# Roots of the q/kv statistics on ScalarE, and a new order of the stage's last steps

## The chip, the cores and the metric

The kernel runs on one core of one Trainium2 chip. The metric is device time in microseconds (us) for one execution of the whole program. Five engines work from queues of their own, each in its order: TensorE (PE: matmuls and transposes), VectorE (DVE), ScalarE (ACT), GpSimd (POOL), and SyncE (SP), which issues DMAs. An instruction that needs the result of another engine waits at the head of its queue, and everything behind it on that engine waits with it.

## The reference

One layer with two parallel groups of heads that read the same normalised input. There are 1024 latent tokens and 128 context tokens, 9 tiles of 128 rows; the context is tile 8. The part that the change touches makes, for each tile, a low-rank query `c_q` (256 wide), a key/value latent `c_kv` (128) and a rotary key (64):

```python
def _rmsnorm(x, g):
    xf = x.astype(jnp.float32)
    y = xf * lax.rsqrt(jnp.mean(xf * xf, axis=-1, keepdims=True) + EPS)
    return (y * g.astype(jnp.float32)).astype(x.dtype)
...
    u, v, g_a, c_q, c_kv, k_rope, g_b = _split_in(h @ w_in)
    a_out = _chunk_mlp(u, v, w_s, b_s, g_v) * jax.nn.silu(g_a)
    q = (_rmsnorm(c_q, q_norm_g) @ w_uq).reshape(B, L, MLA_HEADS, QK_NOPE + QK_ROPE)
    ckv = _rmsnorm(c_kv, kv_norm_g)
```

Keys and values come from `ckv`; attention is a softmax over latent keys and 256 cached context keys for latent tokens, and over the context's own 128 keys for tile 8. The kernel folds the key expansion into the query, so that the normalised latent itself serves as key, and it applies the root of `c_q` later, as the scale of the softmax (`scl`, `nscl`).

## The kernel before

Matmuls are made in three passes on operands that are split into a high part and the low rest. So nearly every result in PSUM is evicted twice: ACT copies the high part, then DVE subtracts it from the PSUM value to give the low part (`lo_of`, line 104). Here such a pair is called an eviction; `kch`/`kcl`, `krh`/`krl`, `cqh`/`cql` are such pairs.

The q/kv stage (lines 986 to 1040) stands between the channel matmuls and attention. Its engines run in the order in which the code issues instructions, and that order is written out by hand: `run((cost, fn))` calls a step's function and moves a planned clock on by its cost; `later(dt, fn)` puts a function on a list with a due time, and `catch_up` issues what is due, in order of due times, before the next step. An eviction that is due earlier on this planned clock thus stands earlier in its engine's queue, whenever its input really comes. `need(...)` issues what is on the list until the named thing has been made.

For each tile t, eight `z_chunk` steps (24 matmuls) accumulate `c_q`, `c_kv` and the rotary key in one PSUM bank. The last one calls `z_stats` (line 824). There ACT copies the bank to SBUF (`z`, line 869), two ACT activations square and sum it (lines 832 and 833), `scales` (line 835) computes 1/sqrt of both sums, and `apply` writes the normalised latent `kvn` and the scales. Before the change, 1/sqrt is an integer first guess and three Newton steps, twelve small DVE operations one after another (`rsqrt_ops`, line 109). For the last tile (`last`, t = 8) squares and scales have later due times (2.6 and 4.2 instead of 0.35 and 1.6), and the operations a wider gap.

Beside the chunks of tile t run steps of earlier tiles: `cq_transpose(t-1)`, `q_rope(t-2)` with its rotation, `q_rope_T(t-3)`, `fold`, and `q_nope(g, h)`, the queries of three tiles and one head. After tile 8's last chunk comes the list of lines 1022 to 1038: transposes of the keys of tiles 0 to 7 (`keys(0, 4, kind)`, `keys(4, 4, kind)`; kind 0 is the latent, 1 the rotary key), `cq_transpose(8)`, `q_rope_T(6)` and `(7)`, `q_rope(8)`, the last query group `q_nope(2, 0..3)`, and tile 8's own `q_rope_T(8)` and `keys(8, 1, kind)`.

PSUM has eight banks. In this stage two belong to a pool `pst` (tag `t`: key transposes of tiles 0 to 3 and of tile 8, `q_rope_T(8)`), six to a pool `psa` (tag `acc`: nearly all else). Within a pool the next tile takes the bank that was given back first, and its first matmul waits for the last reader of the tile before. In attention the six banks go to `o` and the context's own score (one bank), to `s2` (one), and to two score tiles of two banks each. The first score (line 1087, head 0 of tile 0) thus takes over two banks of the stage's last `acc` tiles. The scores of tile 0 need the keys of tiles 0 to 7 and the cached context, not those of tile 8; these are read by the context's own score, which is the fifth step of attention.

The activation tables: ACT works with one set of functions at a time, and the program has a table load (`ACT_TABLE_LOAD`) ahead of each activation whose function is not in the set in force. `warm_e` (line 989) is an activation whose result nobody reads; it is the first ACT instruction of the stage's code and has no input but a constant.

Of the kernel before, what the change touches and what calls it, by code (L numbers as in the profile page):

```python
# [9 lines left out]
F32 = mybir.dt.float32  # L10
# [3 lines left out]
AF = mybir.ActivationFunctionType  # L14
# [4 lines left out]
P = 128  # L19
NT = 9  # L20
# [66 lines left out]
def tile_hymba_step(ctx: ExitStack, tc: tile.TileContext, I, O):  # L87
# [21 lines left out]
    def rsqrt_ops(pool, v, n, tag):  # L109
        r = pool.tile([P, n], F32, tag=f"{tag}r", name=f"{tag}r")  # L110
        t = pool.tile([P, n], F32, tag=f"{tag}t", name=f"{tag}t")
        w = pool.tile([P, n], F32, tag=f"{tag}w", name=f"{tag}w")
        ops = [
            lambda: V.tensor_scalar(t.bitcast(I32), v.bitcast(I32), 1, None, op0=ALU.logical_shift_right),
            lambda: V.tensor_scalar(r.bitcast(I32), t.bitcast(I32), -1, 0x5F3759DF, op0=ALU.mult, op1=ALU.add),
            lambda: V.tensor_scalar(w, v, -0.5, None, op0=ALU.mult),
        ]
        for _ in range(3):
            if n == 1:
                ops.append(lambda: V.scalar_tensor_tensor(t, r, r, w, op0=ALU.mult, op1=ALU.mult))  # L120
            else:
                ops.append(lambda: V.tensor_tensor(t, r, r, op=ALU.mult))
                ops.append(lambda: V.tensor_tensor(t, t, w, op=ALU.mult))
            ops.append(lambda: V.scalar_tensor_tensor(r, t, 1.5, r, op0=ALU.add, op1=ALU.mult))
        return r, ops
# [33 lines left out]
    def later(dt, fn):  # L159
        waiting.append((now[0] + dt, fn))  # L160
        waiting.sort(key=lambda w: w[0])

    def catch_up(until):
        at_ = now[0]
        while waiting and waiting[0][0] <= until:
            due, fn = waiting.pop(0)
            now[0] = due
            fn()
        now[0] = at_
# [29 lines left out]
    def run(step):  # L199
        catch_up(now[0])  # L200
        step[1]()
        now[0] += step[0]
# [621 lines left out]
    def z_stats(t, ps):  # L824
        zt[t] = zp.tile([P, 448], F32, tag="z", name=f"z{t}", bufs=2)
        zs = zt[t]
        ssz = sm.tile([P, 2], F32, tag="ssz", name=f"ssz{t}")
        kr = zs[:, 384:448]

        def squares():  # L830
            j1 = sm.tile([P, 256], BF16, tag="j1", name=f"j1{t}", bufs=1)
            S.activation(j1, ps[:, 0:256], AF.Square, accum_out=ssz[:, 0:1])
            S.activation(j1[:, :128], ps[:, 256:384], AF.Square, accum_out=ssz[:, 1:2])

        def scales():
            v = sm.tile([P, 2], F32, tag="zv", name=f"zv{t}")
            r, ops = rsqrt_ops(sm, v, 2, "z")
            V.tensor_scalar(v[:, 0:1], ssz[:, 0:1], 1.0 / 256.0, EPS, op0=ALU.mult, op1=ALU.add)
            V.tensor_scalar(v[:, 1:2], ssz[:, 1:2], 1.0 / 128.0, EPS, op0=ALU.mult, op1=ALU.add)
            gap = 0.28 if t == NT - 1 else 0.2  # L840
            for i, op in enumerate(ops):
                later(gap * i, op)
            later(gap * len(ops), lambda: apply(r))

        def apply(r):
            V.scalar_tensor_tensor(kvn[:, t, :], zs[:, 256:384], r[:, 1:2], kvg, op0=ALU.mult, op1=ALU.mult)
            V.tensor_scalar(scl[:, t : t + 1], r[:, 0:1], ATTN_SCALE, None, op0=ALU.mult)
            V.tensor_scalar(nscl[:, t : t + 1], r[:, 0:1], -ATTN_SCALE, None, op0=ALU.mult)
            made.add(("k", t))
            if t == NS:  # L850
                nc.sync.dma_start(O["new_ckv"], kvn[:, t, :])
                nc.sync.dma_start(O["new_krope"], kr)

        def rope_key():
            if t < NS:
                t1 = sm.tile([P, 64], F32, tag="kr1", name=f"kr1{t}")
                t2 = sm.tile([P, 64], F32, tag="kr2", name=f"kr2{t}")
                G.tensor_tensor(t1, kr, rope[:, 0, t, :], op=ALU.mult)
                G.tensor_tensor(t2[:, 0:32], kr[:, 32:64], rope[:, 1, t, 0:32], op=ALU.mult)
                G.tensor_tensor(t2[:, 32:64], kr[:, 0:32], rope[:, 1, t, 32:64], op=ALU.mult)  # L860
                G.tensor_tensor(krd[:, t, 0, :], t1, t2, op=ALU.add)
                G.tensor_tensor(krd[:, t, 1, :], t1, t2, op=ALU.add)
            else:
                G.tensor_copy(krd[:, t, 0, :], kr)
                G.tensor_copy(krd[:, t, 1, :], kr)


        last = t == NT - 1
        later(0.3, lambda: S.copy(zs, ps[:, :448]))
        later(2.6 if last else 0.35, squares)  # L870
        later(0.9, rope_key)
        later(4.2 if last else 1.6, scales)

    def cq_transpose(t):
        last = t == NT - 1
# [18 lines left out]
    def q_nope(g, h):  # L894
        need(*[("cq", t) for t in range(3 * g, 3 * g + 3)])
        ps = psa.tile([P, 512], F32, tag="acc", name=f"qn{g}{h}")
        gc = slice(g * GW, (g + 1) * GW)
        passes3(ps[:, :GW], [(wfh[:, q, h, :], wfl[:, q, h, :], cqh[:, q, gc], cql[:, q, gc]) for q in range(2)])
        later(1.2, lambda: S.copy(qnh[g][:, h, :], ps[:, :GW]))
        later(1.75, lambda: lo_of(qnl[g][:, h, :], ps[:, :GW], qnh[g][:, h, :]))  # L900
# [85 lines left out]
    NOPES = {4: [(0, 0)], 5: [(0, 1), (0, 2)], 6: [(0, 3)], 7: [(1, 0), (1, 1)], 8: [(1, 2), (1, 3)]}  # L986
    with tc.manual_schedule(engines=engines):
        warm_e = sm.tile([P, 1], F32, tag="warm", name="warm_e", bufs=1)
        S.activation(warm_e, ones[:, 0:1], AF.Exp)
        rope_weights()  # L990
        for t in range(NT):
            beside = []
            if t >= 2:
                beside.append((0.75, lambda t=t: q_rope(t - 2)))
            beside += [(1.05, lambda n=n: q_nope(*n)) for n in NOPES.get(t, [])[:1]]
            if t >= 1:
                beside.append((0.25, lambda t=t: cq_transpose(t - 1)))
            if 1 <= t < 5:
                beside.append((0.45, lambda t=t: fold(t - 1)))
            if t >= 3:  # L1000
                beside.append((0.45, lambda t=t: q_rope_T(t - 3)))
            beside += [(1.05, lambda n=n: q_nope(*n)) for n in NOPES.get(t, [])[1:]]
            if t == NT - 1:
                beside.append((0.75, lambda: q_rope(t - 1)))
            merged([(0.62, lambda t=t, k=k: z_chunk(t, k)) for k in range(NK)], beside)
        closed(c_w1)
        c_kv, kv = opened("kv", side="left")
        kch = kv.tile([P, 11 * P], F32R, tag="kch", name="kch")
        kcl = kv.tile([P, 11 * P], F32R, tag="kcl", name="kcl")
        krh = kv.tile([P, 11 * P], F32R, tag="krh", name="krh")  # L1010
        krl = kv.tile([P, 11 * P], F32R, tag="krl", name="krl")
        vh = kv.tile([P, 11, P], F32R, tag="vh", name="vh")
        vl = kv.tile([P, 11, P], F32R, tag="vl", name="vl")
        for i, (dh, dl) in enumerate(((kch, kcl), (krh, krl))):
            later(0.3, lambda dh=dh, i=i: pool_copy(dh[:, CTX0:], ctxr[:, i, :]))
            later(0.3, lambda dh=dh, dl=dl, i=i: G.tensor_tensor(dl[:, CTX0:], ctxr[:, i, :], f32(dh[:, CTX0:]), op=ALU.subtract))
        cv = [v_[:, 9:, :].rearrange("p a r -> p (a r)") for v_ in (vh, vl)]
        later(11.0, lambda: pool_copy(cv[0], ctxr[:, 2, :]))
        later(11.0, lambda: G.tensor_tensor(cv[1], ctxr[:, 2, :], f32(cv[0]), op=ALU.subtract))
        for t0, c in ((8, 1), (0, 4), (4, 4)):  # L1020
            later(11.5, lambda t0=t0, c=c: values(t0, c))
        for cost, fn in (
            (0.45, lambda: keys(0, 4, 0)),
            (0.45, lambda: keys(0, 4, 1)),
            (0.25, lambda: cq_transpose(8)),
            (0.45, lambda: keys(4, 4, 0)),
            (0.45, lambda: keys(4, 4, 1)),
            (0.45, lambda: q_rope_T(6)),
            (0.45, lambda: q_rope_T(7)),
            (0.75, lambda: q_rope(8)),  # L1030
            (1.05, lambda: q_nope(2, 0)),
            (1.05, lambda: q_nope(2, 1)),
            (1.05, lambda: q_nope(2, 2)),
            (0.15, lambda: keys(8, 1, 1)),
            (1.05, lambda: q_nope(2, 3)),
            (0.25, lambda: q_rope_T(8)),
            (0.15, lambda: keys(8, 1, 0)),
        ):
            run((cost, fn))
        catch_up(1e9)  # L1040
    closed(c_zp)
    closed(c_pa)
# [565 lines left out]
```

## Time and profile before

| | us |
|---|---|
| median of three runs | 635.0 (634.12 to 635.34) |
| the profiled execution | 633.38 |
| its span, first to last instruction | 631.6 |
| q/kv stage on PE, first chunk to first score | 247.56 to 325.29 |

The mean granted clock of TensorE over the span is 0.995 of full speed. The profile is one execution; a row of a timeline has start, duration, engine, line of the kernel, operation, output<-inputs, shape and count, and in brackets the engine's idle time just before with what ended it. Durations of successive matmuls overlap, so the pace of PE is read from start to start. A low part has line 104 whatever it belongs to, so it is told by its tile names; `area` holds the finished queries. A row of `x2` or `x4` joins neighbours of one form.

### The profile page before, as it was taken

The page shows a single profiled execution, that of the slowest core. Times are in us where ns is not written, and L with a number is a line of the kernel's source. Part 1 is how long each engine was busy: PE and PEld are TensorE (multiplying, and loading weights), DVE is VectorE, ACT ScalarE, POOL GpSimd, SP SyncE. Part 2 cuts the span into 40 slices and gives each one's busy share as a digit, 9 for nine tenths or more (in the row PEclk, how much of TensorE's full clock was granted, in tenths as well). Part 3 has the DMA queues.
Part 4 walks back from the last instruction along what each step waited for, and adds up shares of the span by engine and source line. Part 5 has one row for each costly group of instructions (what it writes and reads, how often), then busy time and mean ns, then how long its engine had stood idle before and what let it go on. Part 6 is the DMA issues. An engine that isn't in the chain of part 4 may idle for free.

```text
span 631.6 us, 9907 instructions
## 1 busy us (share of the span) xinstructions
PE 614.2 (97%) x3733; PEld 557.1 (88%) x3733; DVE 366.5 (58%) x907; ACT 259.4 (41%) x615; POOL 181.8 (29%) x217
## 2 busy tenths in 40 slices
PE   7999999999999999999979999999999999999995
PEld 6677889999999999999967999999999988888884
DVE  3666447048556200667866665776766755487655
ACT  8456753112111111455646556555555543132212
POOL 2545123247532510433443221332222341000001
PEclk9999999999999999999989999999999999999999
DMA  8993100042322320000010000000101012524311
GB/s 324 353 356 107 34 0 2 1 141 109 113 92 72 110 88 13 25 2 1 2 39 1 2 2 0 1 1 35 34 1 34 33 68 87 181 100 134 104 64 66
DMA packets 17120, 46.32 MB, mean 73 GB/s; under 512 B 1953, under 2 KB 6449, under 8 KB 17073
## 3 DMA queue, kind: packets, MB, share of 16 engines
q1 hardware_dynamic: 16928, 45.51, 21.1%
q8 instruction: 29, 0.48, 0.3%
q10 hardware_dynamic: 144, 0.20, 0.1%
q14 instruction: 19, 0.15, 0.1%
HBM read 40.87 MB, written 4.83 MB: 72 GB/s over the span
## 4 chain that ended last, share of the span: by engine, by line
PE 91%; DVE 4%; ACT 2%; DMA 1%; issue 1%; SPq 0%; ACTq 0%
PE tp L670 6%; PE tp L150 6%; PE tp L152 6%; PE tp L151 6%; PE pT L1134 5%; PE w L1383 5%; PE w L1382 5%; PE w L1381 5%; PE s L1087 3%; PE o L1158 3%; PE o L1160 3%; PE s L1088 3%; PE s L1089 3%; PE s L1090 3%; PE o L1159 3%; PE s L1091 3%
## 5 line engine op out<-in xcount | busy, mean ns | idle before, releaser
L104 DVE TENSOR_TENSOR pl<-pT,ph 128x512 fp32r<-128x512 f32 x81 | 55.5, 687 | 48.0 <-ACT ph L1138 47.8
L1078 POOL TENSOR_SCALAR e<-e,rs 128x1280 f32<-128x1280 f32 x32 | 43.0, 1343 | 134.1 <-DVE rs L1077 116.3
L152 PE MATMUL tp<-area,w2l 128*128 128x384 f32 x216 | 72.5, 336 | 0.0
L150 PE MATMUL tp<-area,w2h 128*128 128x384 f32 x216 | 72.5, 336 | 0.0
L151 PE MATMUL tp<-area,w2h 128*128 128x384 f32 x216 | 72.5, 336 | 0.0
L1072 ACT ACTIVATE e<-s,nb,scl 128x256 f32<-128x256 f32 x64 | 56.1, 881 | 37.6 <-DVE nb L1066 37.6
L1138 ACT CAST ph<-pT 128x512 fp32r<-128x512 f32 x80 | 45.4, 589 | 43.5 <-PE pT L1134 40.6
L1134 PE MATMUL pT<-ident,e 128*128 128x128 f32 x320 | 47.8, 272 | 0.7 <-DVE pl L104 0.7
L1158 PE MATMUL o<-ph,vh 128*128 128x256 f32 x160 | 47.8, 299 | 0.0
L104 DVE TENSOR_TENSOR w2l<-w2r,w2h 128x1024 fp32r<-128x1024 f32 x12 | 20.2, 1685 | 46.1 <-POOL w2h L107 46.1
L1160 PE MATMUL o<-ph,vl 128*128 128x256 f32 x160 | 44.9, 281 | 0.0
L1159 PE MATMUL o<-pl,vh 128*128 128x256 f32 x160 | 44.7, 280 | 0.0
L1383 PE MATMUL w<-area,ml 128*128 128x512 f32 (+1 forms) x114 | 43.2, 379 | 0.0
L1134 PEld LDWEIGHTS pT<-ident,e 128*128 128x128 f32 x320 | 37.5, 140 | 4.4 <-DVE pl L104 1.5
L1062 DVE TENSOR_REDUCE m<-s 128x1 f32<-128x1024 f32 x32 | 38.9, 1216 | 4.0 <-PE s L1091 4.0
L150 PEld LDWEIGHTS tp<-area,w2h 128*128 128x128 f32 x216 | 40.5, 188 | 0.6 <-issue 0.5
L151 PEld LDWEIGHTS tp<-area,w2h 128*128 128x128 f32 x216 | 40.5, 188 | 0.2
L152 PEld LDWEIGHTS tp<-area,w2l 128*128 128x128 f32 x216 | 40.5, 188 | 0.0
L1087 PE MATMUL s<-kch,area 128*128 128x512 f32 (+2 forms) x100 | 39.5, 395 | 0.6 <-DVE area L104 0.6
L670 PE MATMUL tp<-area,w2h 128*128 128x384 f32 x144 | 37.4, 340 | 0.0
L1089 PE MATMUL s<-kch,area 128*128 128x512 f32 (+2 forms) x100 | 35.8, 358 | 0.0
L1088 PE MATMUL s<-kcl,area 128*128 128x512 f32 (+2 forms) x100 | 35.7, 357 | 0.0
(309 smaller groups left out, 1590.0 us busy)
## 6 DMA issues: line engine op xcount, KB each, us to landing
ada<-in_ada_ss SPq DMA_DIRECT2D x16, 512.0 KB, 10.9
w2r<-in_w_t SPq DMA_DIRECT2D x12, 512.0 KB, 4.3
xr<-in_x SPq DMA_DIRECT2D x9, 512.0 KB, 5.1
adag<-in_ada_g SPq DMA_DIRECT2D x8, 512.0 KB
wor<-in_w_o SPq DMA_DIRECT2D x8, 512.0 KB, 3.4
out_y<-y SPq DMA_DIRECT2D x8, 512.0 KB, 2.7
x<-in_x SPq DMA_DIRECT2D x6, 512.0 KB, 8.7
wvr<-in_w_v SPq DMA_DIRECT2D x8, 256.0 KB, 8.6
```

The source lines that it names most:

```text
L104: V.tensor_tensor(lo, src, f32(hi), op=ALU.subtract)
L150: T.matmul(ps, wh, xh, start=j == 0, stop=False)
L151: T.matmul(ps, wh, xl, start=False, stop=False)
L152: T.matmul(ps, wl, xh, start=False, stop=j == n - 1)
L670: T.matmul(tps[i, g][:, :GW], w_[i][:, k, :], x_[k, g], start=k == 0 and j == 0, stop=k == NK - 1 and j == 2)
L1072: S.activation(e[:, sl], src, AF.Exp, bias=nb, scale=scl[:, t : t + 1], accum_out=su[:, i : i + 1])
L1087: T.matmul(ps, qh_, kch[:, sl], start=True, stop=False)
L1134: T.transpose(ps[:, w : w + P], es[t, h][:, c * P : (c + 1) * P], ident)
L1158: T.matmul(o, vh[:, kt, :], ph[:, sl], start=c == 0, stop=False)
L1159: T.matmul(o, vh[:, kt, :], pl[:, sl], start=False, stop=False)
L1160: T.matmul(o, vl[:, kt, :], ph[:, sl], start=False, stop=c == n - 1)
L1383: T.matmul(ps, b, woh[k][:, c0:c1], start=False, stop=k == NK - 1)
```

## The change

In `scales`, ACT takes the square roots of both sums (one activation each, with the mean's factor as scale and EPS as bias), and DVE takes the reciprocal and makes one Newton step on it, four operations instead of twelve. The last tile's squares and scales lose their later due times; scales are due at 1.5 instead of 1.6 for all tiles. In the list after the last chunk, `keys(8, 1, 1)` and `keys(8, 1, 0)` go from behind `q_nope(2, 2)` and from the end to a place behind `q_nope(2, 0)`, and `q_rope_T(8)` goes ahead of `q_nope(2, 3)`. The unread activation at the stage's start asks for Sqrt instead of Exp, and a second one at its end asks for Exp.

```diff
@@ scales @@
             v = sm.tile([P, 2], F32, tag="zv", name=f"zv{t}")
-            r, ops = rsqrt_ops(sm, v, 2, "z")
-            V.tensor_scalar(v[:, 0:1], ssz[:, 0:1], 1.0 / 256.0, EPS, op0=ALU.mult, op1=ALU.add)
-            V.tensor_scalar(v[:, 1:2], ssz[:, 1:2], 1.0 / 128.0, EPS, op0=ALU.mult, op1=ALU.add)
-            gap = 0.28 if t == NT - 1 else 0.2
-            for i, op in enumerate(ops):
-                later(gap * i, op)
-            later(gap * len(ops), lambda: apply(r))
+            root = sm.tile([P, 2], F32, tag="zw", name=f"zw{t}")
+            r = sm.tile([P, 2], F32, tag="zr", name=f"zr{t}")
+            u = sm.tile([P, 2], F32, tag="zt", name=f"zt{t}")
+            for i, width in enumerate((256.0, 128.0)):
+                c_ = slice(i, i + 1)
+                S.activation(root[:, c_], ssz[:, c_], AF.Sqrt, bias=epsb, scale=1.0 / width)
+                V.tensor_scalar(v[:, c_], ssz[:, c_], 1.0 / width, EPS, op0=ALU.mult, op1=ALU.add)
+            steps_ = [
+                lambda: V.reciprocal(r, root),
+                lambda: V.tensor_tensor(u, r, r, op=ALU.mult),
+                lambda: V.scalar_tensor_tensor(u, u, -0.5, v, op0=ALU.mult, op1=ALU.mult),
+                lambda: V.scalar_tensor_tensor(r, u, 1.5, r, op0=ALU.add, op1=ALU.mult),
+            ]
+            for i, op in enumerate(steps_):
+                later(0.35 + 0.2 * i, op)
+            later(0.35 + 0.2 * len(steps_), lambda: apply(r))
@@ z_stats @@
-        last = t == NT - 1
         later(0.3, lambda: S.copy(zs, ps[:, :448]))
-        later(2.6 if last else 0.35, squares)
+        later(0.35, squares)
         later(0.9, rope_key)
-        later(4.2 if last else 1.6, scales)
+        later(1.5, scales)
@@ the stage @@
-        S.activation(warm_e, ones[:, 0:1], AF.Exp)
+        S.activation(warm_e, ones[:, 0:1], AF.Sqrt)
@@ the list after the last chunk @@
             (1.05, lambda: q_nope(2, 0)),
+            (0.15, lambda: keys(8, 1, 1)),
+            (0.15, lambda: keys(8, 1, 0)),
             (1.05, lambda: q_nope(2, 1)),
             (1.05, lambda: q_nope(2, 2)),
-            (0.15, lambda: keys(8, 1, 1)),
+            (0.25, lambda: q_rope_T(8)),
             (1.05, lambda: q_nope(2, 3)),
-            (0.25, lambda: q_rope_T(8)),
-            (0.15, lambda: keys(8, 1, 0)),
         ):
             run((cost, fn))
+        later(0.6, lambda: S.activation(warm_e, ones[:, 0:1], AF.Exp))
         catch_up(1e9)
```

## The prediction

> **What bounds the kernel now.** I read the page first: who is busy over the span.
>
> ```profile
> span 631.6 us, 9907 instructions
> ...
> PE 614.2 (97%) x3733; PEld 557.1 (88%) x3733; DVE 366.5 (58%) x907; ACT 259.4 (41%) x615; POOL 181.8 (29%) x217
> ```
>
> TensorE (PE) is busy for 97% of the span, so an edit on DVE or ACT is worth only the PE idle time that it ends. The second view is that of the waits, narrowed to PE between 225 and 350 us; two of its four rows lie where the diff works, at the end of the q/kv stage:
>
> ```profile
> PE kT L959 <- DVE krl L104: 3.8, 1, 3.8
> PE s L1087 <- DVE area L104: 0.6, 1, 0.6
> ```
>
> The third view is PE's timeline there (start, duration, what ran, idle time before it in brackets).
>
> ```profile
> 312.05 0.60 PE L959 MATMUL kT<-ident,kvn 128*128 128x128 f32 x4
> ...
> 314.69 0.38 PE L939 MATMUL qrT<-ident,qun 128*128 128x128 f32 x2
> 315.02 0.38 PE L150 MATMUL qr<-wrh,cqh 128*128 128x256 f32 x1
> ...
> 315.84 0.34 PE L150 MATMUL qn<-cqh,wfh 128*128 128x384 f32 x1
> ...
> 316.88 0.33 PE L150 MATMUL qn<-cqh,wfh 128*128 128x384 f32 x1
> ...
> 318.97 0.27 PE L959 MATMUL kT<-ident,krd 128*128 128x128 f32 x1
> ...
> 320.15 0.38 PE L939 MATMUL qrT<-ident,qun 128*128 128x128 f32 x2
> 324.36 0.33 PE L959 MATMUL kT<-ident,kvn 128*128 128x128 f32 x1 [3.83 <-DVE krl L104]
> 325.29 0.80 PE L1087 MATMUL s<-kch,area 128*128 128x512 f32 x1 [0.60 <-DVE area L104]
> ...
> 329.25 0.27 PE L1087 MATMUL s<-kch,area 128*128 128x256 f32 x1
> ...
> 329.84 0.39 PE L1087 MATMUL s<-kch,area 128*128 128x512 f32 x1
> ...
> 330.99 0.22 PE L1087 MATMUL s<-kch,area 128*128 128x128 f32 x1
> ```
>
> PE has nothing to do from 320.53 until tile 8's key (kT from kvn) can be transposed at 324.36, and waits once more before the first score at 325.29. The first score, ten matmuls, then takes 3.96 us (325.29 to 329.25), although five of the same shape take 1.15 us a moment later (329.84 to 330.99). The fourth view, windows of 3.41 us, shows why:
>
> ```profile
> 7.82:11.23 3.41, 1.67 (x22) 0.75 (x20) 1.58 (x6) 2.52 (x5) 0.90 (x1) 1.00 1.01 365
> ...
> 318.43:321.84 3.41, 2.10 (x14) 1.79 (x12) 3.13 (x10) 1.71 (x5) 0.00 (x0) 1.00 0.00 0
> 321.84:325.26 3.42, 0.33 (x1) 0.14 (x1) 3.27 (x14) 0.53 (x2) 1.11 (x3) 1.00 0.07 19
> 325.26:328.67 3.41, 3.38 (x8) 2.71 (x9) 1.01 (x3) 1.65 (x2) 3.24 (x4) 0.50 0.56 163
> ```
>
> The first number after the comma is PE's busy time; the granted clock is the third from the end. A window with 0.33 us of PE work is followed by one at clock 0.50; windows with 1.67 and 2.10 us of work are not. So the idle time costs twice: 3.83 + 0.60 us of waiting, and 3.96 - 2 x 1.15 = 1.66 us of slow matmuls.
>
> What PE waits for is on DVE.
>
> ```profile
> 313.35 0.69 DVE L104 TENSOR_TENSOR kcl<-kT,kch 128x512 fp32r<-128x512 f32 x1 [0.76 <-ACT kch L962]
> 313.96 0.68 DVE L104 TENSOR_TENSOR krl<-kT,krh 128x512 fp32r<-128x512 f32 x1
> 314.56 0.41 DVE L104 TENSOR_TENSOR cql<-cqT,cqh 128x256 fp32r<-128x256 f32 x1
> ...
> 317.39 0.68 DVE L949 TENSOR_TENSOR area<-qrT,area 64x512 fp32r<-64x512 f32 x1 [0.85 <-ACT area L948]
> 318.09 0.15 DVE L838 TENSOR_SCALAR zv<-ssz 128x1 f32<-128x1 f32 x1
> ...
> 323.44 0.15 DVE L124 SCALAR_TENSOR_TENSOR zr<-zt,zr 128x2 f32<-128x2 f32 x1
> 323.63 0.35 DVE L846 SCALAR_TENSOR_TENSOR kvn<-z,zr,kvg 128x128 f32<-128x128 f32 x1
> ...
> 324.02 0.28 DVE L104 TENSOR_TENSOR krl<-kT,krh 128x128 fp32r<-128x128 f32 x1
> 324.22 1.01 DVE L104 TENSOR_TENSOR area<-qn,area 128x384 fp32r<-128x384 f32 x2
> ```
>
> Tile 8's statistics begin at 318.09 and leave the Newton chain at 323.60; behind it in DVE's order stand kvn, the low part krl of tile 8's rope key, which gives back the PSUM bank that the last transpose needs, and the low parts of the last query groups, one of which frees a bank of the first score.
>
> **The change, part by part.** I lay the new order of the `later` due times on the start-to-start times of these rows. Laid on the old order, the same method gives 324.47 for the key's transpose and 325.41 for the first score, 0.1 late.
>
> Tiles 0 to 7: twelve chained DVE operations become four (about 0.19 us each, 323.44 to 323.63), ACT gets two Sqrt. The waits view has no PE wait in these tiles (its other two rows lie after 342 us), so I count nothing. The cover that this needs is thinnest in tile 0, where the first Sqrt brings a table load:
>
> ```profile
> 2.25 1.28 ACT L989 ACT_TABLE_LOAD   x1
> ...
> 253.92 0.36 ACT L886 CAST cqh<-cqT 128x256 fp32r<-128x256 f32 x1
> ...
> 254.75 0.41 DVE L104 TENSOR_TENSOR cql<-cqT,cqh 128x256 fp32r<-128x256 f32 x1
> ...
> 258.88 0.28 PE L150 MATMUL qr<-wrh,cqh 128*128 128x256 f32 x1
> ```
>
> The warm-up activation of L989 ran at 2.25 us, not at the stage's start: it depends on nothing and was drawn to the front. I expect the same of the Sqrt that takes its place, so the table in force at 254 is still Silu's, and a load stands before tile 0's first root. With 1.28 us for it and 0.5 for two roots, cqh of tile 0 moves from 253.92 to 255.7 and cql ends near 256.6; PE wants it at 258.88. 2.3 us are left. The Exp load at the stage's other end falls into ACT's wait for the first scores, as now. Both cost 0; without that cover, up to 1.3 us each.
>
> Tile 8: squares and scales come at the usual times, ahead of the key evictions.
>
> ```profile
> 312.30 0.53 ACT L869 COPY z<-zacc 128x448 f32<-128x448 f32 x1 [0.23 <-PE zacc L981]
> 312.73 0.59 ACT L962 CAST kch<-kT 128x512 fp32r<-128x512 f32 x1
> 313.20 0.60 ACT L962 CAST krh<-kT 128x512 fp32r<-128x512 f32 x1
> 313.68 0.40 ACT L886 CAST cqh<-cqT 128x256 fp32r<-128x256 f32 x1
> ...
> 314.43 0.43 ACT L832 ACTIVATE j<-zacc 128x256 bf16<-128x256 f32 x1
> ...
> 315.24 0.58 ACT L962 CAST krh<-kT 128x512 fp32r<-128x512 f32 x1
> ```
>
> ```profile
> L424 ACT ACTIVATE xroot<-ssq,epsb x3: 296/296/296, 9.1 to 45.5; 128x3 f32<-128x3 f32 x3
> ```
>
> The squares take 0.81 us (314.43 to 315.24) and now stand at 312.73; kch follows at 313.5 (0.47), then two roots of 0.30 each, overlapping, done at 314.46. No row shows a 128x1 root; I take the 128x3 one, the nearest. Bounds: 0.15, as a 128x1 operation on DVE (318.09), and 0.43, as ACT's 128x256 square; with two roots either moves what follows by under 0.3 us. On DVE the **reciprocal waits for the second root**, and four things wait behind it that PE needs: kcl 314.7 (now 313.35), 0.60; two Newton operations, 0.40; krl, 0.60; cql from 316.3 to 316.70. That is the new wait: q_rope(8) needs cql and starts at 316.75 instead of 315.02; PE, done at 314.91, idles 1.84 us.
>
> Then PE runs q_rope(8) 0.82 (315.02 to 315.84), q_nope(2,0) 1.05 (315.84 to 316.88), both key transposes 0.22, two groups 2.10: 320.94. kvn is there at 317.2, so the keys cost no wait. Next, q_rope_T(8) reuses the bank of the first key transpose, which krl frees. DVE, from 316.62: last Newton step 0.20, kvn with its two scalings 0.39 (323.63 to 324.02), two 512-wide lows 1.20, four rope lows of 0.71 (317.39 to 318.09), krl at 321.25, done 321.53. PE waits 0.64 us, then q_rope_T 0.22 and q_nope(2,3) 1.05 bring the first score to **322.85, 2.44 us earlier** than 325.29.
>
> Does the score wait again? Banks are handed out in the order in which they are given back. With the old order the first score inherits the bank of q_nope(2,3), and waits. With squares early, tile 8's accumulator comes free sooner, q_rope(8) takes its bank and q_nope(2,3) follows there; that bank goes to the context tokens' own score, which comes only at 326.9. The first score inherits q_rope_T(6) and q_nope(2,0), evicted by 322.0. I count no wait.
>
> Clock: PE now idles 1.84 and 0.64 us, so a window keeps at least 3.41 - 1.84 = 1.57 us of work, next to the 1.67 that held full clock. I take no slow window: 1.66 us less for the first score, rounded 1.62 with 0.234 a matmul.
>
> The three DMAs behind kvn on SP (the two cache outputs, then the first w_o load) leave 6.5 us earlier, POOL's values split as well; none ends a PE wait in this view. SP and POOL: 0.
>
> Sum: 2.44 + 1.62 = **4.06 us**. The profiled execution took 633.38 us, of which 631.6 is span: 629.3. The median of the three timed runs is 635.0 (634.12 to 635.34), 1.6 above it; with the same gain, **630.9 us**, -0.64%.
>
> [...] In the rows, 0.33 us of PE work in 3.42 did not hold the clock. [...]
>
> **Rivals.**
> 1. *The slow clock comes back.* Ahead of the new 1.84 us gap stand 2.86 us of transposes (312.05 to 314.91). If they count as idle, 4.7 us are idle in a row, and a window that falls inside runs q_rope(8) and the groups at half clock: +1.7, gain 2.4, 632.6 us. For: the lone transpose. Against: window phase has to fit (some 1 in 3). Chance 0.12.
> 2. *The first score still waits for the last query group's low part.* It ends at 324.45 in my order: +1.6, gain 2.5, 632.5. For: it is the wait of now. Against: the bank order. 0.09.
> 3. *Little of the new waits comes*, if DVE and ACT run closer than I lay them: both gaps go, gain up to 6.5, 628.5. 0.08.
> 4. *Slower: the coupling costs in every tile.* DVE's reciprocal waits on ACT and holds cql, on which the query matmuls wait. At 1.74 us, tile 8's price, for eight tiles: +13.9 - 4.1, 643 us; it decides from 0.51 us a tile. Against: in tiles 0 to 7 q_rope comes two tiles later (254.75 to 258.88 in tile 0), in tile 8 at once. 0.04.
> 5. *The edit doesn't do what it says*: the early roots end behind the same key evictions, krl still closes the chain at 324, and the gain is under 1.2 us. 0.06.
>
> **How the numbers follow.** Forecast 0.61 (gain 3.3 to 4.9: 630.1 to 631.7); the rest as above. A measurement of this kernel tells 0.2%, 1.3 us, from no change. Rivals 1 to 3 are faster as well: 0.90 in all, less 0.02 for 1 and 2 together (gain 0.8): faster 0.88; with rival 5, same 0.08; rival 4, slower 0.04. The range takes in rivals 1 and 2 with some spread and the near part of rival 3: 628.9 to 633.1.
>
> **What would show it.** PE's row qr at L150 with 1.5 to 2 us of idle time put down to DVE L104; kT of kvn with none; q_rope_T(8) with about 0.6, from krl; the first score near 322.9, ten matmuls in 2.4 us, granted clock 1.00 throughout; a Sqrt table load at about 254 us and none near 248. Wrong would be: a 0.50 window after 315, a wait at the first score, or waits at qr or qn in tiles 0 to 7.

## The result, and the profile after

| | before | after |
|---|---|---|
| median of 11 runs each, us | 634.97 (634.12 to 636.95) | 632.35 (629.84 to 633.87) |
| the profiled execution, us | 633.38 | 633.54 |
| first key transpose of the list to first score, us | 13.24 | 11.46 |
| the first score's ten matmuls, us | 3.96 | 2.31 |
| sum of the last two (called L below), us | 17.20 | 13.77 |

The ratio of after to before, from runs on the same chips, is 0.9944, with a 95% interval of 0.9928 to 0.996: 3.6 us faster (2.5 to 4.6). The two medians differ by 2.6 only, because after's lies at the edge between two groups of its runs (below). The forecast was 4.06 us and 630.9.

The two profiled executions are equally long all the same. The page of after says so first:

```profile
span 631.5 us, 9855 instructions
```

A span can be cut into three pieces: up to the first key transpose of the list, L, and the rest. The rest is 302.35 us in both (before 631.6 - 329.25, after 631.5 - 329.15), and L is 3.43 us shorter. The first piece is 3.33 us longer, 315.38 against 312.05, and all of that arises ahead of the q/kv stage: its first chunk starts at 250.88 against 247.56, and from there to the first key transpose it is 64.50 us in after and 64.49 in before. The windows of after (PE's busy time first, the granted clock third from the end) show what happened there:

```profile
7.83:11.25 3.42, 1.51 (x22) 0.72 (x20) 1.58 (x6) 2.53 (x5) 0.93 (x1) 0.99 1.01 368
11.25:14.66 3.41, 2.88 (x19) 2.28 (x12) 0.42 (x1) 1.63 (x5) 1.93 (x2) 0.50 1.04 422
14.66:18.07 3.41, 3.41 (x14) 3.12 (x14) 1.89 (x5) 3.29 (x7) 0.00 (x0) 0.51 1.03 404
...
317.20:320.60 3.40, 2.24 (x17) 1.80 (x16) 2.71 (x8) 3.39 (x10) 3.15 (x8) 1.00 0.03 7
320.60:324.00 3.40, 3.40 (x21) 3.20 (x20) 3.37 (x8) 2.56 (x7) 3.00 (x5) 1.00 0.12 31
324.00:327.40 3.40, 2.25 (x14) 1.84 (x13) 3.35 (x8) 1.57 (x4) 1.96 (x3) 1.00 0.00 0
```

This execution ran at half clock from 11.25 to 18.07, some 240 us before the stage begins. The change does not touch that place. Of after's eleven runs five have a mean clock of 0.997 or 0.998 and took 629.84 to 630.47 us; the other six have 0.991 to 0.995 and took 632.35 to 633.87. The profiles of the experiments below agree: r1, r5 and r7 have a half clock there too and reach the first chunk at 249.90 to 250.65; those with the same start and without it do so at 247.42 to 248.10. So the total carries a part that comes and goes at the program's start, and the comparisons below go by L, with the total beside it. In the stage itself (the last three windows) the clock is 1.00, as forecast.

The waits view of after, PE between 225 and 350 us, has none of before's rows at the stage's end (kT from krl, s from area) and three new ones:

```profile
PE qrT L946 <- DVE krl L104: 1.2, 1, 1.2
PE qr L152 <- DVE cql L104: 1.0, 1, 1.0
...
PE qr L150 <- ACT cqh L893: 0.2, 1, 0.2
```

PE's timeline of after has them in place (the first row is tile 0's q_rope, the others are the list after the last chunk):

```profile
262.21 0.28 PE L150 MATMUL qr<-wrh,cqh 128*128 128x256 f32 x1
...
315.38 0.60 PE L966 MATMUL kT<-ident,kvn 128*128 128x128 f32 x4
...
318.59 0.39 PE L150 MATMUL qr<-wrh,cqh 128*128 128x256 f32 x1 [0.19 <-ACT cqh L893]
318.81 0.28 PE L151 MATMUL qr<-wrl,cqh 128*128 128x256 f32 x1
320.06 0.38 PE L152 MATMUL qr<-wrh,cql 128*128 128x256 f32 x1 [0.97 <-DVE cql L104]
...
321.79 0.27 PE L966 MATMUL kT<-ident,kvn 128*128 128x128 f32 x1
...
325.52 0.44 PE L946 MATMUL qrT<-ident,qun 128*128 128x128 f32 x2 [1.15 <-DVE krl L104]
...
326.84 0.39 PE L1095 MATMUL s<-kch,area 128*128 128x512 f32 x1
...
329.15 0.28 PE L1095 MATMUL s<-kch,area 128*128 128x256 f32 x1
```

Tile 8's key is transposed at 321.79 without a wait, and the first score starts at 326.84 without one. PE idles 0.19 + 0.97 us in q_rope(8) and 1.15 us at q_rope_T(8), instead of 3.83 and 0.60.

The two longer of the new waits are for DVE. Its timeline in after, from the reciprocal to the low part of tile 8's rope key:

```profile
317.82 0.17 DVE L845 RECIPROCAL zr<-zw 128x2 f32<-128x2 f32 x1 [0.70 <-ACT zw L842]
317.90 0.67 DVE L104 TENSOR_TENSOR kcl<-kT,kch 128x512 fp32r<-128x512 f32 x1
318.49 0.22 DVE L846 TENSOR_TENSOR zt<-zr 128x2 f32<-128x2 f32 x1
318.74 0.33 DVE L847 SCALAR_TENSOR_TENSOR zt<-zt,zv 128x2 f32<-128x2 f32 x1
...
319.93 0.32 DVE L848 SCALAR_TENSOR_TENSOR zr<-zt,zr 128x2 f32<-128x2 f32 x1
320.29 0.92 DVE L855 SCALAR_TENSOR_TENSOR kvn<-z,zr,kvg 128x128 f32<-128x128 f32 x1
...
325.17 0.29 DVE L104 TENSOR_TENSOR krl<-kT,krh 128x128 fp32r<-128x128 f32 x1
```

`kvn` takes 0.92 us, 0.97 with its two scalings; the prediction laid 0.39 for these, and 0.20 from one Newton operation to the next, on rows of 0.35 and 0.15 in before. In the same stretch GpSimd splits the cached context, which is due there in both kernels; in before, tile 8's statistics came after that work. GpSimd's timeline in after:

```profile
317.97 0.72 POOL L1023 TENSOR_TENSOR kcl<-ctxr,kch 128x256 fp32r<-128x256 f32 x1
318.67 0.40 POOL L107 TENSOR_SCALAR krh<-ctxr 128x256 fp32r<-128x256 f32 x1
319.15 0.72 POOL L1023 TENSOR_TENSOR krl<-ctxr,krh 128x256 fp32r<-128x256 f32 x1
319.84 0.40 POOL L107 TENSOR_SCALAR vh<-ctxr 128x256 fp32r<-128x256 f32 x1
320.33 0.73 POOL L1026 TENSOR_TENSOR vl<-ctxr,vh 128x256 fp32r<-128x256 f32 x1
```

The DVE operations that grew have two inputs in SBUF. They end about when a GpSimd operation beside them ends: `zt` at 319.07 with `krh`, `zr` at 320.25 with `vh` (320.24), `kvn` at 321.21, 0.15 us after `vl`. Those that also read PSUM (`kcl<-kT,kch`, 0.67) did not grow.

ACT's timeline in after shows the table loads and tile 0's root:

```profile
2.25 1.28 ACT L996 ACT_TABLE_LOAD   x1
...
257.37 1.28 ACT L842 ACT_TABLE_LOAD   x1
258.66 0.48 ACT L842 ACTIVATE zw<-ssz,epsb 128x1 f32<-128x1 f32 x2
259.05 0.35 ACT L893 CAST cqh<-cqT 128x256 fp32r<-128x256 f32 x1
...
327.54 1.28 ACT L1047 ACT_TABLE_LOAD   x1
...
331.26 0.56 ACT L1080 ACTIVATE e<-s,nb,scl 128x256 f32<-128x256 f32 x1 [2.22 <-DVE nb L1074]
```

### The profile page after: what moved, and what is told of

It is laid out like the page before. It is cut to its first block, busy times and chain, and to the rows that moved or that the text cites. A ratio compares the mean times of both kernels' runs of the same rounds, so it can differ in the third digit from the quotient of the medians.

```text
span 631.5 us, 9855 instructions
## 1 busy us (share of the span) xinstructions
PE 615.5 (97%) x3733; PEld 558.3 (88%) x3733; DVE 359.0 (57%) x835; ACT 264.2 (42%) x635; POOL 175.2 (28%) x217
## 4 chain that ended last, share of the span: by engine, by line
PE 90%; DVE 3%; DMA 3%; ACT 3%; SPq 1%; issue 1%; ACTq 0%
PE tp L670 6%; PE tp L151 6%; PE tp L150 6%; PE tp L152 6%; PE pT L1142 5%; PE w L1389 5%; PE w L1390 5%; PE w L1391 5%; PE o L1166 3%; PE o L1168 3%; PE o L1167 3%; PE s L1097 3%; PE s L1098 3%; PE s L1096 3%; PE s L1095 3%; PE s L1099 3%
## 5 line engine op out<-in xcount | busy, mean ns | idle before, releaser
L1098 PE MATMUL s<-krh,area 128*128 128x512 f32 (+2 forms) x100 | 35.4, 354 | 0.0
```

## The experiments

The theory: the early roots take the idle time before tile 8's key and with it the half clock, and what is left is DVE's order behind them. The rivals: the new order of the list does it; the slow first score has another cause than the idle time, or transposes don't hold the clock; the waits that are left come from ACT or from the order, not from DVE's operations. All numbers at a glance; "start" is the first key transpose to the first score, "score" its ten matmuls, both from one profiled execution, and the ratio is to before with its 95% interval.

| run | start | score | L | median total | ratio |
|---|---|---|---|---|---|
| before | 13.24 | 3.96 | 17.20 | 634.97 | |
| after | 11.46 | 2.31 | 13.77 | 632.35 | 0.9944 (0.9928 to 0.996) |
| r1_roots_only | 11.17 | 2.38 | 13.55 | 631.26 | 0.993 (0.9907 to 0.9954) |
| r2_order_only | 18.45 | 2.41 | 20.86 | 639.73 | 1.0059 (1.0038 to 1.0079) |
| r3_no_tables | 11.47 | 2.31 | 13.78 | 633.05 | 0.9952 (0.9932 to 0.9972) |
| r4_filled_gap | 13.35 | 2.38 | 15.73 | 632.42 | 0.9965 (0.9944 to 0.9987) |
| r9_filled_tr | 13.34 | 2.40 | 15.74 | 633.03 | 0.9964 (0.9944 to 0.9985) |
| r5_t_last | 10.63 | 2.40 | 13.03 | 632.06 | 0.9937 (0.9913 to 0.996) |
| r6_pool_late | 10.48 | 2.28 | 12.76 | 631.16 | 0.9924 (0.9897 to 0.995) |
| r7_cql_first | 11.20 | 2.28 | 13.48 | 633.03 | 0.9943 (0.9922 to 0.9964) |
| r8_start_warm | 11.46 | 2.28 | 13.74 | 631.38 | 0.9932 (0.9912 to 0.9953) |
| r10_comb_a | 9.63 | 2.40 | 12.03 | 628.55 | 0.9891 (0.9869 to 0.9913) |
| r11_comb_b | 9.35 | 2.39 | 11.74 | 630.42 | 0.9916 (0.9891 to 0.9942) |
| r12_comb_c | 9.35 | 2.38 | 11.73 | 629.71 | 0.9905 (0.9884 to 0.9926) |

### Which part of the change does it

r1 has the roots and the early due times, with before's list and before's table lines; r2 has the new list alone; r3 is after with the table lines of before.

```diff
--- r1_roots_only: after with
-        S.activation(warm_e, ones[:, 0:1], AF.Sqrt)
+        S.activation(warm_e, ones[:, 0:1], AF.Exp)
...
-            (0.15, lambda: keys(8, 1, 1)),
-            (0.15, lambda: keys(8, 1, 0)),
             (1.05, lambda: q_nope(2, 1)),
             (1.05, lambda: q_nope(2, 2)),
-            (0.25, lambda: q_rope_T(8)),
+            (0.15, lambda: keys(8, 1, 1)),
             (1.05, lambda: q_nope(2, 3)),
+            (0.25, lambda: q_rope_T(8)),
+            (0.15, lambda: keys(8, 1, 0)),
...
-        later(0.6, lambda: S.activation(warm_e, ones[:, 0:1], AF.Exp))
```

> The roots on ScalarE and the usual due times of tile 8, with the old order of the list and the old place of the Exp load. L is the time from the first key transpose of the list to the end of the first score: 17.20 us before (312.05 to 329.25), 13.77 after (315.38 to 329.15). Theory (the gain is PE's wait for DVE plus the half clock that follows it, and the early statistics alone remove both): L between 13.2 and 14.0, total about 3.5 us under before, like after. Rival (the new order of the list is what pays): L over 15.5, total less than 1.5 us under before.

> The new order of the list alone, with the old Newton chain and its late due times. Theory: PE meets tile 8's key 3.4 us earlier in its queue and stands before it 6 to 7 us, since kvn still comes near 323.5; the first score starts about 3.4 us later than before and at half clock; L about 20.6, total 3 to 4 us over before. Rival (the order pays by itself): L under 16, total 1 us or more under before.

> After, with both table edits undone: the unread activation at the stage's start asks for Exp again, none stands at its end. Theory: the Exp load falls into ScalarE's wait for the first scores (2.2 us idle in after) and the first Sqrt loads its table near tile 0 in either case: L as after (13.8), total as after within 0.3 us. Rival (the load moved to the end pays): the first exp of attention 1.3 us later, total up to 1.3 us over after.

r1 has the whole gain: L is 13.55, 0.22 below after. With the old list, tile 8's key comes last, and PE waits 0.7 us there in place of q_rope_T(8). The waits of r1:

```profile
PE qr L152 <- DVE cql L104: 1.0, 1, 1.0
PE kT L966 <- DVE krl L104: 0.7, 1, 0.7
```

r2, the new order without the early roots, costs 3.66 us of L and is slower in total. Its PE timeline, the two rows that wait:

```profile
324.08 0.47 PE L959 MATMUL kT<-ident,kvn 128*128 128x128 f32 x1 [6.53 <-DVE kvn L846]
...
330.88 0.50 PE L1087 MATMUL s<-kch,area 128*128 128x512 f32 x1 [1.43 <-DVE area L104]
```

The late `kvn` now stands ahead of three query groups, which could have run in its shadow. PE's idle time costs clock here too, but not where it was expected: the clock is 0.50 from 320.97 to 327.80, under the query groups, and the score itself takes 2.41 us at full clock. So the order isn't a gain of its own: it is only affordable with the early roots, and beside them it loses 0.2 us of L. r3's L is after's to 0.01. Without the load at the stage's end the Exp load stands behind the wait for `nb`, and the first exponential starts 3.39 us after the end of the first score (326.37 to 329.76) instead of 2.11 in after (329.15 to 331.26); the rest of r3's span, from the first score's end, is 302.33 us against 302.35. So that 1.3 us on ACT is hidden, and the table edits are worth nothing here. r3's median is 0.7 us over after's, more than the 0.3 expected; its two runs with a clock of 0.997 (630.36 and 630.59) lie beside after's five, so that is the start as well.

### Is the slow score the idle time's doing, and do transposes count

Both kernels are before with work put into PE's idle time ahead of tile 8's key: constants are multiplied (r4) or transposed (r9), and nobody reads the result.

```diff
+    def fillers(n):
+        ps = psa.tile([P, 512], F32, tag="acc", name="filler")
+        for _ in range(n):
+            T.matmul(ps[:, 0:P], ident, ones, start=True, stop=True)     # r4
+            T.transpose(ps[:, 0:P], ones, ident)                         # r9
...
             (0.25, lambda: q_rope_T(8)),
+            (0.0, lambda: fillers(13)),     # r9: fillers(28)
             (0.15, lambda: keys(8, 1, 0)),
```

> Before, with 13 matmuls on constants (about 0.24 us each, result unread) ahead of the last key transpose, where PE had nothing to do for 3.83 us. Nothing else is moved. Theory (the slow first score is the clock that fell in the idle window): the score starts as before, 13.2 us after the first key transpose, but its ten matmuls take 2.3 us instead of 3.96; L about 15.6, total 1.6 us under before. Rival (the score is slow for another reason, such as its operands or PSUM): L 17.2 and the total of before.

> Before, with 28 transposes of constants (about 0.11 us each, result unread) in the place of the 13 matmuls of the filled gap. It tells whether transposes hold the clock: PE is as busy as with the matmuls, but only with transposes. Theory (they count as work, by the windows of after, where 2.9 us of transposes and 1 us of idle time cost nothing): the first score takes 2.3 us, L 15.7, total 1.6 us under before. Rival (they do not count): granted clock 0.50 from the first score on, score 3.9 us, L 17.2, total as before.

In r4 the first score starts as late as in before (13.35 against 13.24 after the first key transpose) and takes 2.38 us instead of 3.96. The idle time alone made it slow. In r9 the same work is transposes only. Its PE timeline, then its windows:

```profile
320.24 3.22 PE L989 MATMUL filler<-ident,ones 128*128 128x128 f32 x28
324.25 0.33 PE L959 MATMUL kT<-ident,kvn 128*128 128x128 f32 x1 [0.79 <-DVE krl L104]
```

```profile
321.43:324.84 3.41, 2.36 (x20) 1.93 (x18) 3.21 (x15) 0.23 (x2) 0.80 (x3) 1.00 0.02 6
324.84:328.26 3.42, 3.00 (x16) 2.58 (x17) 1.72 (x5) 1.95 (x4) 3.25 (x4) 1.00 0.62 176
```

The window from 321.43 to 324.84 holds nothing but transposes (the fillers' rest and tile 8's key), 2.36 us of them; the stretches are as long as the steps in which the recorded clock changed (0.50 for 3.41 us from 325.26 in before, for twice that from 11.25 in after). The window behind it has clock 1.00, where before's, behind 0.33 us of work, had 0.50. In this run transposes held the clock. Whether they would also raise a halved clock no run here shows.

### What the new waits consist of

r6 puts GpSimd's context splits behind tile 8's values. r5 puts q_rope_T(8) behind the last query group. r7 gives tile 8's squares and scales later due times, so that kcl, krl and cql go ahead of them.

```diff
--- r6_pool_late: after with
+        later(11.0, lambda: values(8, 1))
...
-            later(0.3, lambda dh=dh, i=i: pool_copy(dh[:, CTX0:], ctxr[:, i, :]))
+            later(11.1, lambda dh=dh, i=i: pool_copy(dh[:, CTX0:], ctxr[:, i, :]))
...
-        for t0, c in ((8, 1), (0, 4), (4, 4)):
+        for t0, c in ((0, 4), (4, 4)):
--- r5_t_last: after with
-            (0.25, lambda: q_rope_T(8)),
             (1.05, lambda: q_nope(2, 3)),
+            (0.25, lambda: q_rope_T(8)),
--- r7_cql_first: after with
-        later(0.35, squares)
+        later(2.0 if t == NT - 1 else 0.35, squares)
...
-        later(1.5, scales)
+        later(2.5 if t == NT - 1 else 1.5, scales)
```

> After, with GpSimd's splits of the cached context (keys, rope keys, values) queued behind the split of tile 8's values, so that GpSimd waits for kvn of tile 8 instead of working beside it. Theory (kvn took 0.92 us instead of 0.35 and two Newton operations 0.2 to 0.3 instead of 0.16 because both engines read SBUF at the time): kvn of tile 8 at 0.35 us, the chain of DVE 0.6 us shorter, L about 13.2. Rival (kvn is slow for another reason, such as its place behind a PSUM read): kvn stays near 0.9, L stays 13.8.

> After, with q_rope_T(8) moved behind q_nope(2, 3). Theory (in after it stands 1.15 us before the bank that krl of tile 8 holds, and 1.05 us of matmuls can run in that time): its wait falls to about 0.2 us, the first score may then wait up to 0.3 us for the low part of q_nope(2, 0); L from 13.8 to about 13.0, total 0.8 us under after in runs of equal clock. Rival (DVE's queue sets the end, whatever the order on PE): L stays at 13.5 or more.

> After, with tile 8's squares due at 2.0 and its scales at 2.5, so that on DVE the first key lows and cql stand ahead of the reciprocal. Theory: the wait of q_rope(8) for cql (0.2 + 1.0 us) goes, but tile 8's key transpose now waits about 1.5 us for kvn: the wait moves, since DVE's work ahead of krl of tile 8 is the same; L about 13.4, 0.3 under after. Rival (the reciprocal's wait on ScalarE is the price of the change): L under 12.8.

r6, DVE's timeline over the same operations as shown of after:

```profile
314.47 0.17 DVE L845 RECIPROCAL zr<-zw 128x2 f32<-128x2 f32 x1 [0.70 <-ACT zw L842]
314.55 0.67 DVE L104 TENSOR_TENSOR kcl<-kT,kch 128x512 fp32r<-128x512 f32 x1
315.14 0.15 DVE L846 TENSOR_TENSOR zt<-zr 128x2 f32<-128x2 f32 x1
315.32 0.16 DVE L847 SCALAR_TENSOR_TENSOR zt<-zt,zv 128x2 f32<-128x2 f32 x1
...
316.52 0.35 DVE L855 SCALAR_TENSOR_TENSOR kvn<-z,zr,kvg 128x128 f32<-128x128 f32 x1
...
320.83 0.29 DVE L104 TENSOR_TENSOR krl<-kT,krh 128x128 fp32r<-128x128 f32 x1
```

With GpSimd away, `kvn` is back at 0.35 and the Newton operations at 0.15 and 0.16. From the reciprocal to krl it is 6.36 us, against 7.35 in after (317.82 to 325.17): 0.57 of the 0.99 lie in `kvn` and 0.42 in the Newton operations ahead of it, where 0.6 in all was expected. L falls by 1.01. That the collision with GpSimd lengthened the chain is thus shown by taking it away. Not every operation grew beside GpSimd. `kvn`, with two inputs in SBUF, took 0.92 against 0.35 us, but kcl, with one input in PSUM, took 0.67 in both kernels, although in after GpSimd's L1023 ran beside it from 317.97. An operation with one input in SBUF, `zv<-ssz` at 316.57 in after, took its usual 0.15 us beside GpSimd's `qr<-qr,qr` (316.43 to 317.16). Why they differ no run here shows.

r5 takes 0.74 us off L: the last query group covers most of the wait for krl, of which 0.2 us are left. r7 shows that the wait can be moved but not removed by order. Its waits:

```profile
PE kT L966 <- DVE kvn L855: 1.8, 1, 1.8
PE qrT L946 <- DVE krl L104: 0.6, 1, 0.6
```

q_rope(8) no longer waits; the key transposes wait 1.8 us instead, and the first score comes only 0.26 us earlier. What counts is how much DVE has to do ahead of krl.

### The program's start, and the combinations

r8 gives PE more unread work at the program's start. r10 joins r5 and r6, r11 adds r7, and r12 adds r8.

```diff
--- r8_start_warm: after with
-        keep_warm(24)
+        keep_warm(28)
```

> After, with 28 instead of 24 matmuls on constants at the program's start; nothing near the q/kv stage changes, L 13.8. Theory (after's profile has clock 0.50 from 11.2 to 18.1 us, behind a window with 1.49 us of PE work; before's has full clock behind one with 1.67; runs of after come at a mean clock of 0.997 near 630.3 us or at 0.991 to 0.995 between 632.3 and 633.9): with 0.9 us more of PE work in that window no run falls under 0.996, all near 630.2, median 2 us under after's. Rival (the two groups of runs come from elsewhere): both groups stay.

> After, with q_rope_T(8) behind q_nope(2, 3) and with GpSimd's context splits behind tile 8's values. Theory (the two gains are on one chain and add up but for the low part of q_nope(2, 0)): L 12.1 to 12.4, no wait over 0.3 us but that for cql (0.7), total 1.4 to 1.6 us under after at equal clock. Rival (what remains is bound by DVE's total work): L 12.7.

> As the combination before it, with tile 8's squares due at 2.0 and scales at 2.5, so that cql stands ahead of the reciprocal. Theory: PE's wait for cql goes, the key transpose waits about 1 us for kvn instead, and DVE starts its backlog earlier: L 11.6 to 12.0. Rival (it moves a wait as it did alone): L as in the combination before it.

> As the second combination, with 28 instead of 24 matmuls on constants at the start. Theory: L as there; no run under a mean clock of 0.996; all times within 628 to 630.5, the fastest median of the study. Rival (the added matmuls cost as much as the clock at the start gives): median as of the second combination or over it.

r8 did what it should to the clock: all six runs have 0.996 to 0.998. But they took 630.55 to 632.72 us, not the 629.84 to 630.47 of after's runs at that clock. Its profiled execution reaches the first key transpose at 313.32, between after's 315.38 and before's 312.05, with a mean clock of 0.997. Its q/kv stage starts at 248.82, and that of r12, which has 28 matmuls as well, at 249.38, both later than in every profile with 24 and no half clock there (247.42 to 248.10). Around 19 us PE waits for a load of `ada`, 1.15 us in r8 and 0.85 + 0.64 in r12; those others have none there. So far as two profiles show it, the added matmuls cost time where they save clock; why that load comes late stays open.

r10 has the lowest median of all. Its waits:

```profile
PE qr L152 <- DVE cql L104: 0.7, 1, 0.7
...
PE qr L150 <- ACT cqh L893: 0.2, 1, 0.2
```

q_rope_T(8) no longer waits. L is 12.03, which is after's 13.77 less 0.74 and 1.01, to 0.01: the two parts add. The total is 628.55 us, 1.1% below before. That is 3.8 us below after's median, more than the 1.74 of L; the rest is the start, since r10's runs all have a clock of 0.994 to 0.997, and against the median of after's five runs at 0.997 or 0.998, 630.46, it is 1.9. r11 and r12 take another 0.3 us off L, but their totals (630.42 and 629.71, with overlapping intervals) don't tell them from r10. r12 was expected to be the fastest and isn't, though none of its runs is under 0.996.

## Why the prediction was right, point by point

**The gain's two terms.** 1.62 us were forecast for the clock, 1.65 measured; r4 shows the cause. For the earlier first score 2.44 were forecast and 1.78 measured. The mis-sized term is "DVE, from 316.62: last Newton step 0.20, kvn with its two scalings 0.39" with the Newton operations before it: priced from rows in which GpSimd left DVE alone. The collision was worth 0.99 us of the chain (7.35 against 6.36). Some of it was offset, since the rest of the chain had been laid too long: 6.79 us from the reciprocal to krl in the prediction, 6.36 in r6. So q_rope_T(8) waited 1.15 us instead of 0.64, which is 0.51 of the missing 0.66.

The hint was there in before. The operations of its Newton chains on the same tiny shape mostly took 0.15 to 0.16 us, but in each of tiles 1 to 7 one took 0.58 to 0.60, every time beside the same GpSimd operation. Tile 1's, in DVE's timeline of before, and GpSimd's:

```profile
261.39 0.16 DVE L123 TENSOR_TENSOR zt<-zt,zw 128x2 f32<-128x2 f32 x1
261.59 0.58 DVE L124 SCALAR_TENSOR_TENSOR zr<-zt,zr 128x2 f32<-128x2 f32 x1
```

```profile
261.42 0.73 POOL L925 TENSOR_TENSOR qr<-qr,qr 128x256 f32<-128x256 f32 x1
```

The prediction set POOL to 0 because none of its results ends a PE wait. It should have asked as well beside whose operations POOL's now run. In after the same GpSimd operation meets `kvn` in tiles 1 to 7, which takes 0.72 to 0.91 us there; PE has no wait in those tiles, so it costs nothing.

**q_rope(8).** The wait was forecast as 1.84 us, and PE was to start at 316.75; shifted by the 3.33 us of the late start that is 320.08, and the first matmul that needs cql started at 320.06. The time of arrival was right, in part by luck: in r6, without the collision, that matmul starts 4.44 us after the first key transpose, against 4.68 in after and 4.70 in the prediction. But the first of the six matmuls to need cql is the third; two ran ahead from 318.59, and the idle time was 0.19 + 0.97. The step was priced as one block where its operands arrive apart.

**Sqrt.** The unread activation was drawn to 2.25 us, as L989 was, and the real load stands before tile 0's first root, at 257.37. With 3.33 us taken off, that is 254.0, forecast 254. A pair of 128x1 roots takes 0.48 us; 0.5 was taken. cqh followed at 259.05 and q_rope(0) ran at 262.21 without a wait. No wait of PE appeared in tiles 0 to 7, and from the stage's first chunk to the first key transpose it took 64.50 us against 64.49, so rival 4, the slower one, fell: its cover held. (Its price was added up wrongly: 635.0 + 13.9 - 4.1 is 644.8 and not 643, which starts from the profiled 633.38.)

**The rivals.** 1, transposes that don't count: no half clock in the stage, and r9 removes its ground. The prediction's own bound on the clock, at least 1.57 us of work in a window, was not tried, as the stage's windows in after kept 2.24 and more. It was no safe bound: windows with 1.51 and 1.89 us were followed by half clock at the program's start (last section). 2, the first score waiting for the last low part: no wait at 326.84, so the bank order was as laid out. 3, little of the new waits: 2.31 us of them came, 2.48 were forecast. 5, krl still at the end of the chain at 324: it is, and PE waits for it, but in q_rope_T(8), ahead of one query group, and for 1.15 us.

**The new order.** The prediction priced the change as a whole and so didn't see that its second part earns nothing. With the old list r1 is 0.22 us better in L, which is more than the 0.04 by which after, r3 and r8 differ there, though the totals don't tell the two apart.

**The total.** 632.35 lies in the range, 1.4 us above the forecast. 0.63 of that is L (4.06 - 3.43); the rest is the half clock at the start, which came in six of eleven runs and which the prediction didn't consider; the five without it have a median of 630.46. How near the total came is thus in part luck.

## What to carry to other kernels

When work is moved on one engine, look at what it will then stand beside on the others, not only at what it waits for and who waits for it: small VectorE operations with both inputs in SBUF took 1.5 to 4 times as long beside GpSimd's (0.15 to 0.22 and to 0.58 us). Price an idle stretch of TensorE together with the clock that it costs (here 3.83 and 0.60 us of waiting, and a first score of 3.96 instead of 2.38 us), and a waiting step by each matmul's own operands. And split a change with several parts before keeping it: here one part held the gain, one cost 3.7 us of its stretch by itself, and one was worth nothing.

## What the runs showed of the hardware that was not expected

- In r9 transposes held TensorE's clock: behind a window of 3.41 us with 2.36 us of them, and no other work of PE, it was 1.00.
- A window with 1.51 us of PE work (7.83 to 11.25 in after) was followed by half clock, while one with 1.67 (before, the same place) was not. But the time that PE is busy can't be all that decides: in r7 a window with 1.89 us was followed by half clock, as its windows show. Most of that work is matmuls for `modp` on operands of 128*32 or with results of 128x2; whether these count for less was not tried.

```profile
10.06:13.48 3.42, 1.89 (x22) 0.96 (x23) 1.52 (x5) 1.77 (x2) 2.06 (x2) 1.00 1.03 417
13.48:16.89 3.41, 3.41 (x17) 3.31 (x17) 1.28 (x2) 3.17 (x7) 0.80 (x1) 0.50 1.03 415
```

- From run to run the program's start falls to either side, and that moves the stage's start, and with it the total, by 2 to 3 us (249.90 to 250.88 against 247.42 to 248.10), nearly as much as this change.
- A DVE operation on 256 numbers with two inputs in SBUF, 0.15 us long, took 0.33 beside a GpSimd operation of 0.40 us (after) and 0.58 beside one of 0.73 (before); one of 0.35 us took 0.92 beside one of 0.73 (after).
